# Who computes the low halves of the weight blocks: 32 subtractions from GpSimd to VectorE, and two pairs of blocks split later in their norm chain

## The chip, the cores and the metric

One NeuronCore of one Trainium2 chip runs the kernel. The metric is the device time of one execution in microseconds (us). The engines are TensorE (PE, matmuls; PEld its weight loads), VectorE (DVE), ScalarE (ACT), GpSimd (POOL) and SyncE (SP, which issues the loads). Each runs its own instructions in the order in which the program lists them and meets the others through semaphores.

## The reference

Two transformer blocks, all in fp32. The first is a trunk of two layers over 256 latent and 256 context tokens of width 1024:

```python
for i in range(DEPTH):                       # DEPTH = 2
    x, xc = trunk_layer(x, xc, mod, mod_c, p, ang_row, ang_col, last=(i == DEPTH - 1))

# trunk_layer
h = rmsnorm(x, p["g_pre_mix"]) * (1 + sc1) + sh1
u = h @ w_in
y = concatenate([y_sc, y_mla, y_cf, y_na], axis=-1) @ p["w_out"]
x = x + ga1 * rmsnorm(y, p["g_post_mix"])
hm = rmsnorm(x, p["g_pre_mlp"]) * (1 + sc2) + sh2
x = x + ga2 * rmsnorm(sq_relu_mlp(hm, p["w_mlp1"], p["w_mlp2"]), p["g_post_mlp"])
```

The four mixers are a short convolution (sc), a latent attention (mla), a convolution of 31 taps (cf, the "conformer") and an attention over a neighbourhood (na). The context rows xc go the same way in the first layer; in the last layer they give only keys and values. So layer 0 is wide (512 rows) and layer 1 narrow (256 rows). The second block (a differential attention, a dilated attention and a gated MLP) comes after it and is not touched here.

## The kernel before, in words

**Three products for one.** A matmul in fp32 is done as three of a faster type, fp32r: each operand is split into a high half H, the operand rounded to fp32r, and a low half L, operand minus H. `mm3` issues H·H (L430), L·H (L431) and H·L (L432). So every weight block has to be split before PE can use it, and every activation too.

**Weight blocks.** The weights lie in one stream of blocks of 128x1024, in the order of their use. SP fetches two at a time (1 MB, tile raw, four buffers). `step` (L355) takes the next block of the stream, lets ACT write H (L373) and then either POOL or DVE write L:

```python
nc.scalar.activation(hi, t[:, j, :], AF.Copy)
pool = pool or (self.pool_l and len(self.units) % self.pool_l == 0)
(nc.gpsimd if pool else nc.vector).tensor_tensor(lo, t[:, j, :], hi, op=ALU.subtract)
```

`self.pump(upto, pool)` calls `step` until the stream stands at block `upto`; `self.used` is the number of blocks that PE's instructions have taken up so far. What sets the order on an engine is where in the program `pump` is called: the subtraction stands behind all that the program wrote for its engine before.

**Attention** (`attention`, L1506) runs in slots, 19 in layer 0 and 11 in layer 1: one item (a head and 128 or 256 queries) enters per slot. A slot first pumps to `self.used + SLOT_LEAD`, then issues the item's scores and softmax (`attn_scores` or `na_scores`: scores S on PE, maxima mx and the bias nb = mx·nqs on DVE at L1403 and L1404, the exponentials P on ACT at L1412, their reciprocal sum rd and the multiply P·rd on DVE at L1414 and L1415), then the transposes of an earlier item (PT on PE, PTs copied by DVE and ACT), background taps of the convolution (cfacc: half the channels by DVE, L984, half by ACT, cft at L990, and POOL, L991), then "fillers" for PE (the nk, sc_x, sc_b, sc_c and out projections, matmuls that need a split weight block), then the values of the oldest item (PV; its halves yH on ACT, yL on DVE, L467 and L468; one y in layer 1). At slot 0 (`POOL_FROM = 0`) it sets `self.pool_l = 1`, from where on `step` gives every low half to POOL.

**Norm chains.** After the out projection and after the first MLP's second matmul, the rows 0 and 1 are normalized and turned into the operand of the next matmul: `pre_transpose` (L852) transposes xn in eight blocks (hT on PE), forms hF = hT·scale + shift on ACT (L843) or DVE (L845), and `pre_split` writes hH on ACT (L849) and hL on DVE (L850; `pool_free` is off here). After every second block it calls `between(k0)`. In the two wide chains (`block1_wide`, L1990 and L2023) `between` pumps two weight blocks, at k0 == 2, with `pool=ALL`.

**End of the first MLP** (L2035). After the chunks of m2 come in, `self.pool_l = 1` is set and `self.pump(self.used + 5)` splits the blocks of the next layer's first projection (tiles a, g, ag, tok). Later `conformer_in` sets `pool_l` itself between its two halves, and `token_block` clears it.

Of the kernel before, what the change touches and what calls it, by code (L numbers as in the profile page):

```python
# [38 lines left out]
ALL = (1,) * 8  # L39
# [17 lines left out]
TAPS = (3, 3), (4, 4)  # L57
TOK_TAPS = 3, 2
NORM_AT = 0
POOL_FROM = 0  # L60
CF_SLOTS = (7, 9, 12), (5, 7, 9)


# [240 lines left out]
class Program:  # L304
# [1206 lines left out]
    def attention(self, l, sets, y, fillers, steps):  # L1511


        items = [(kind, hd, st) for kind in ("mla", "na") for st in range(sets) for hd in range(4)]
        P, PT, bias, after = {}, {}, {}, []
        n = len(items)
        slots = n + AHEAD + 1
        total, done = sum(f[1] for f in fillers), 0.0
        for i in range(slots):
            if i == POOL_FROM:  # L1520
                self.pool_l = 1
            if fillers and fillers[0][4:]:
                for _, fn in [q for q in after if q[0] == "sc"]:
                    fn()
                after = [q for q in after if q[0] != "sc"]
            if i + 4 < n and items[i + 4][0] == "na" and items[i + 4][2] == 0 and i % 2 == 0:
                bias[i + 4] = [self.na_bias(l, items[i + 4][1] + e) for e in range(2)]
            if i + 1 in bias and i % 2:
                bias[i + 1] = bias[i + 2] = [f() for f in bias[i + 1]]
            self.pump(self.used + SLOT_LEAD)  # L1530
            if i < n:
                kind, *item = items[i]
                P[i] = self.attn_scores(*item) if kind == "mla" else self.na_scores(*item, bias.pop(i, None))
            if 0 <= i - AHEAD < n:
                PT[i - AHEAD] = (self.attn_transpose if items[i - AHEAD][0] == "mla" else self.na_transpose)(P.pop(i - AHEAD))
            self.background(*SLOT_TAPS[l])
            for _, fn in after:
                fn()
            after = []
            while fillers and (i == slots - 1 or fillers[0][2] <= i and all(x != fillers[0][3] for x, _ in after)  # L1540
                               and (done < total * (i + 1) / slots or not fillers[0][1])):
                fn, w, _, kind = fillers.pop(0)[:4]
                while any(x == kind for x, _ in after):
                    after.pop(0)[1]()
                r = fn()
                if r:
                    after.append((kind, r))
                done += w
            if i in steps:
                r = steps[i]()  # L1550
                if r:
                    after.append(("cf", r))
            k = i - AHEAD - 1
            if 0 <= k < n and items[k][0] == "na":
                self.na_values(*items[k][1:], PT.pop(k), y)
            elif 0 <= k < n and items[k][1] % 2:
                self.attn_values(*items[k][1:], [PT.pop(k - 1), PT.pop(k)], y)
            if k == 4 * sets - 1:
                self.KT = self.QT = self.VM = None
        for _, fn in after:  # L1560
            fn()
        self.pool_l = False
        assert not fillers
# [417 lines left out]
    def block1_wide(self, l, y, banks, ga):  # L1981
        v = self.nc.vector
        xn, n = {}, 0
        self.post_half(0, 0, banks.pop(0), ga[0])
        for p in self.out_second("out", OUT_ORDER, y, 4, 2):
            if p is None:
                h = self.new_h()
                self.pool_free = False
                self.pre_transpose([xn[0], xn[1]], *self.affine(l, 1, 0), h, 0,
                                   lambda k0: k0 == 2 and self.pump(self.used + 3, pool=ALL))  # L1990
                self.pool_free = True
                continue
            self.post_half(n, 1, p, ga[n // 2], (2, 3) if n > 1 else None)
            p = None
            if n < 2:
                self.post_end(n)
                xn[n] = self.pre_stats(n)[0]
            n += 1
            if n < 4:
                self.post_half(n, 0, banks.pop(0), ga[n // 2], (2, 3) if n > 1 else None)  # L2000
        self.pump(self.used + 5, pool=ALL)
        self.post_end(2, 3)
        xn[2], xn[3] = self.pre_stats(2, 3)
        ga = []

        hs, h = [h], None

        def ctx(between):
            self.pre_transpose([xn[2], xn[3]], *self.affine(l, 1, 1), hs[0], 256, between)

        n, held = 0, []

        def half(n, p):
            ps, y = p
            v.tensor_tensor(y, ps, y, op=ALU.add)
            self.post_half(n // 2, n % 2, y, ga[n // 4], (2, 3) if n > 3 else None)

        for p in self.mlp_wide(l, hs, ctx, lambda: ga.extend(self.gate_rows(l, 1, 2))):
            if p is None:
                h2 = self.new_h()  # L2020
                self.pool_free = False
                self.pre_transpose([xn[0], xn[1]], *self.affine(l + 1, 0, 0), h2, 0,
                                   lambda k0: k0 == 2 and self.pump(self.used + 3, pool=ALL))  # L2023
                self.pool_free = True
                continue
            if n < 5:
                half(n, p)
            else:
                held.append((n, p))
            p = None  # L2030
            if n in (1, 3):
                self.post_end(n // 2)
                xn[n // 2] = self.pre_stats(n // 2)[0]
            n += 1
        self.pool_l = 1  # L2035
        self.pump(self.used + 5)
        while held:
            half(*held.pop(0))

        def rows():  # L2040
            self.post_end(2, 3)
            xn[2], xn[3] = self.pre_stats(2, 3)

        self.ctx_rows = rows
        self.ctx_part = lambda: self.pre_transpose([xn[2], xn[3]], *self.affine(l + 1, 0, 1), h2, 256)
        return h2
# [438 lines left out]
```

## Time and profile before

| | |
|---|---|
| time, median of 3 runs | 1528.68 us (1526.71 to 1529.3) |
| the profiled execution's own time | 1518.72 us |
| its span, first to last instruction | 1516.8 us |
| mean granted clock of TensorE | 0.986 |
| PE busy | 1438.0 us (95%) |
| VectorE busy | 1030.6 us (68%) |
| ScalarE busy | 764.3 us (50%) |
| GpSimd busy | 566.5 us (37%) |
| low halves (L375) on VectorE | 197, 254.0 us |
| low halves (L375) on GpSimd | 117, 287.7 us |
| high halves (L373) on ScalarE | 314, 317.0 us |

A share is of the span. PE is the engine with hardly any free time, and it works in a fixed order: time is lost where its next instruction's operand is not there. The attention of layer 0 lies at about 133 to 262 us of the span, the first wide norm chain at 286 to 312, the second with the end of the first MLP at 676 to 720, the attention of layer 1 at 751 to 832. The granted clock is the share of TensorE's full speed (2.4 GHz) that the throttle allowed; its lower level is 1.2 GHz.

### The profile page before, as it was taken

Reading aid. Unit: us, or ns where it says so; the run is one execution under the profiler, and the core shown is the slowest. Engines: PE = TensorE matmul, PEld = TensorE weight load, DVE = VectorE, ACT = ScalarE, POOL = GpSimd, SP = SyncE. Lnnn points to the kernel's source line nnn. Section 1 sums busy time; section 2 is a strip of 40 time slices with the busy share of each in tenths; the row PEclk is TensorE's granted clock in tenths of the full one; section 3 lists DMA queues with packets and bytes.
Section 4 is the critical chain, followed back from the end, with each engine's and each line's share of the span. In section 5 each row is a group of like instructions: output and inputs, shape, how many; then the busy total and the mean of one; then the engine's idle time right before and its main releaser. Section 6 shows DMA issues by size and latency. Waiting matters only on the chain.

```text
span 1516.8 us, 21532 instructions
## 1 busy us (share of the span) xinstructions
PE 1438.0 (95%) x8284; PEld 1198.5 (79%) x8284; DVE 1030.6 (68%) x1636; ACT 764.3 (50%) x1398; POOL 566.5 (37%) x348
## 2 busy tenths in 40 slices
PE   8979999999989999998899999998999999899997
PEld 6756767888768878877677789986888998689896
DVE  5697673666988776788775665556566667756655
ACT  4445664565453223345666554454544663555553
POOL 2384631204543501016263400004022555737982
PEclk9999999999999999998999999999999999999999
DMA  9643621124444554634332455464645432644551
GB/s 339 226 176 139 139 102 72 56 84 166 158 171 172 196 169 179 214 137 146 95 74 97 145 182 192 169 203 162 211 167 171 140 134 86 216 137 161 189 185 56
DMA packets 72974, 235.64 MB, mean 155 GB/s; under 512 B 13472, under 2 KB 14120, under 8 KB 72872
## 3 DMA queue, kind: packets, MB, share of 16 engines
q1 hardware_dynamic: 72152, 233.58, 45.2%
q8 instruction: 65, 1.06, 0.3%
q10 hardware_dynamic: 720, 0.69, 0.1%
q14 instruction: 37, 0.30, 0.1%
HBM read 233.20 MB, written 1.05 MB: 154 GB/s over the span
## 4 chain that ended last, share of the span: by engine, by line
PE 65%; DVE 19%; ACT 8%; issue 5%; POOL 2%; DMA 1%; SPq 0%; DVEq 0%; ACTq 0%; POOLq 0%
PE m L431 7%; PE m L432 7%; PE m L430 7%; DVE L L375 3%; PE acc L430 3%; PE acc L431 3%; PE acc L432 3%; PE pj L430 2%; PE pj L431 2%; PE pj L432 2%; ACT H L373 2%; DVE cfacc L984 2%; POOL L L375 2%; PE up L432 2%; PE up L431 2%
## 5 line engine op out<-in xcount | busy, mean ns | idle before, releaser
L375 POOL TENSOR_TENSOR L<-raw,H 128x1024 fp32r<-128x1024 f32 x117 | 287.7, 2483 | 322.4 <-ACT H L373 303.8
L373 ACT ACTIVATE H<-raw 128x1024 fp32r<-128x1024 f32 x314 | 317.0, 1048 | 117.1 <-DMA raw<-in_wst 37.3
L375 DVE TENSOR_TENSOR L<-raw,H 128x1024 fp32r<-128x1024 f32 x197 | 254.0, 1317 | 73.6 <-ACT H L373 71.4
L367 POOL TENSOR_TENSOR uL<-raw,uH 128x512 fp32r<-128x512 f32 x32 | 46.3, 1478 | 193.5 <-ACT uH L366 193.4
L431 PE MATMUL m<-L,hidH 128*128 128x512 f32 x256 | 101.7, 397 | 9.7 <-DVE L L375 9.7
L431 PE MATMUL m<-hL,H 128*128 128x512 f32 (+1 forms) x304 | 108.6, 357 | 2.0 <-DVE hL L850 1.9
L432 PE MATMUL m<-hH,L 128*128 128x512 f32 (+1 forms) x304 | 108.4, 356 | 1.3 <-DVE L L375 1.3
L430 PE MATMUL m<-hH,H 128*128 128x512 f32 (+1 forms) x304 | 108.5, 357 | 1.0 <-ACT hH L849 1.0
L1771 ACT ACTIVATE rl<-m 128x512 f32<-128x512 f32 (+1 forms) x56 | 28.2, 504 | 152.5 <-PE m L432 152.5
L679 POOL TENSOR_TENSOR macc<-mt,macc 128x512 f32<-128x512 f32 x42 | 70.5, 1706 | 92.4 <-ACT mt L677 92.4
L430 PE MATMUL m<-H,hidH 128*128 128x512 f32 x256 | 101.3, 396 | 0.0
L432 PE MATMUL m<-H,hidL 128*128 128x512 f32 x256 | 100.3, 392 | 0.0
L1778 DVE TENSOR_TENSOR rl<-rl 128x512 f32<-128x512 f32 (+1 forms) x56 | 32.2, 575 | 93.1 <-ACT hid L1777 57.0
L683 DVE SCALAR_TENSOR_TENSOR macc<-raw,csil,macc 128x512 f32<-128x512 f32 x98 | 93.5, 1011 | 0.0
L991 POOL TENSOR_TENSOR cfacc<-cft,cfacc 128x512 f32<-128x512 f32 (+1 forms) x60 | 70.6, 1176 | 59.4 <-ACT cft L990 55.6
L432 PE MATMUL up<-h,L 128*128 128x256 f32 x288 | 81.7, 284 | 1.7 <-POOL L L375 1.7
L430 PE MATMUL up<-h,H 128*128 128x256 f32 x288 | 81.7, 284 | 0.0
L431 PE MATMUL up<-h,H 128*128 128x256 f32 x288 | 81.5, 283 | 0.0
L431 PEld LDWEIGHTS m<-L,hidH 128*128 128x128 f32 x256 | 48.4, 189 | 23.8 <-DVE L L375 14.2
L431 PEld LDWEIGHTS m<-hL,H 128*128 128x128 f32 x304 | 57.4, 189 | 10.8 <-DVE hL L850 2.6
L432 PEld LDWEIGHTS m<-hH,L 128*128 128x128 f32 x304 | 57.4, 189 | 10.3 <-DVE L L375 2.2
L430 PEld LDWEIGHTS m<-hH,H 128*128 128x128 f32 x304 | 57.4, 189 | 9.2 <-ACT hH L849 1.2
(533 smaller groups left out, 4112.3 us busy)
## 6 DMA issues: line engine op xcount, KB each, us to landing
raw<-in_wst SPq DMA_DIRECT2D x208, 1024.0 KB
mod<-in_wmod SPq DMA_DIRECT2D x16, 256.0 KB
X<-in_x SPq DMA_DIRECT2D x4, 512.0 KB
nab<-in_rpb SPq DMA_DIRECT2D x32, 64.0 KB
raw<-in_wst SPq DMA_DIRECT2D x2, 512.0 KB
wuq<-in_small SPq DMA_DIRECT2D x4, 256.0 KB
cst<-in_c SPq DMA_DIRECT2D x4, 256.0 KB
grow<-in_rows SPq DMA_DIRECT2D x4, 256.0 KB
```

Source lines behind the costliest of these rows:

```text
L367: nc.gpsimd.tensor_tensor(lo, src, hi, op=ALU.subtract)
L373: nc.scalar.activation(hi, t[:, j, :], AF.Copy)
L375: (nc.gpsimd if pool else nc.vector).tensor_tensor(lo, t[:, j, :], hi, op=ALU.subtract)
L430: mm(out, a[0], b[0], start=start, stop=False)
L431: mm(out, a[0], b[1], start=False, stop=False)
L432: mm(out, a[1], b[0], start=False, stop=stop)
L679: nc.gpsimd.tensor_tensor(o, t, o, op=ALU.add)
L683: v.scalar_tensor_tensor(o, a, c, o, op0=ALU.mult, op1=ALU.add)
L984: v.scalar_tensor_tensor(acc, src, w, acc, op0=ALU.mult, op1=ALU.add)
L991: nc.gpsimd.tensor_tensor(acc, t, acc, op=ALU.add)
L1771: nc.scalar.activation(r[:, :T], ps[:, :T], AF.Relu)
L1778: v.tensor_tensor(r[:, :T], r[:, :T], r[:, :T], op=ALU.mult)
```

## The change

`POOL_FROM` and the line that sets `pool_l` at slot 0 of each attention are removed: the low halves that `step` issues in the slots go to VectorE. In the two wide norm chains `between` pumps at k0 == 6, the last call, and not at k0 == 2, and without `pool=ALL`: ACT's two copies and the two subtractions come at the chain's end, the subtractions on VectorE. At the end of the first MLP `pool_l` is no longer set.

```diff
--- before.py
+++ after.py
@@ -57,7 +57,6 @@
 TAPS = (3, 3), (4, 4)
 TOK_TAPS = 3, 2
 NORM_AT = 0
-POOL_FROM = 0
 CF_SLOTS = (7, 9, 12), (5, 7, 9)
 
 
@@ -1517,8 +1516,6 @@
         slots = n + AHEAD + 1
         total, done = sum(f[1] for f in fillers), 0.0
         for i in range(slots):
-            if i == POOL_FROM:
-                self.pool_l = 1
             if fillers and fillers[0][4:]:
                 for _, fn in [q for q in after if q[0] == "sc"]:
                     fn()
@@ -1987,7 +1984,7 @@
                 h = self.new_h()
                 self.pool_free = False
                 self.pre_transpose([xn[0], xn[1]], *self.affine(l, 1, 0), h, 0,
-                                   lambda k0: k0 == 2 and self.pump(self.used + 3, pool=ALL))
+                                   lambda k0: k0 == 6 and self.pump(self.used + 3))
                 self.pool_free = True
                 continue
             self.post_half(n, 1, p, ga[n // 2], (2, 3) if n > 1 else None)
@@ -2020,7 +2017,7 @@
                 h2 = self.new_h()
                 self.pool_free = False
                 self.pre_transpose([xn[0], xn[1]], *self.affine(l + 1, 0, 0), h2, 0,
-                                   lambda k0: k0 == 2 and self.pump(self.used + 3, pool=ALL))
+                                   lambda k0: k0 == 6 and self.pump(self.used + 3))
                 self.pool_free = True
                 continue
             if n < 5:
@@ -2032,7 +2029,6 @@
                 self.post_end(n // 2)
                 xn[n // 2] = self.pre_stats(n // 2)[0]
             n += 1
-        self.pool_l = 1
         self.pump(self.used + 5)
         while held:
             half(*held.pop(0))
```

Counted by its instructions, 32 subtractions of 128x1024 go from POOL to DVE: 15 in the attention of layer 0, 2 in each norm chain, 3 at the end of the first MLP and at the convolution's first half after it, 10 in the attention of layer 1. The orders on PE and of SP's loads stay; ACT's changes in the two norm chains alone. The rows below have the line numbers of their own kernel; those of the changed kernel are one lower in the rows shown (L374 there is L375 in the profile).

VectorE in the attention of layer 0, two slots near its start (147.6 to 159.4 us of the span before). L, raw and H are a weight block's low half, its fetched form and its high half. Before:

```order
L1414 RECIPROCAL rd_1523<-den_1511 128x2
L1415 TENSOR_SCALAR P_1519<-P_1519,rd_1523 128x512
L984 SCALAR_TENSOR_TENSOR cfacc_886<-cfz_0_883,cfw_639,cfacc_886 128x512 x3
L1403 TENSOR_REDUCE mx_1595<-S_1598 128x1
L1403 TENSOR_REDUCE mx_1595<-S_1600 128x1
L1404 TENSOR_TENSOR nb_1596<-mx_1595,nqs_1320 128x2
L1414 RECIPROCAL rd_1609<-den_1597 128x2
L1415 TENSOR_SCALAR P_1605<-P_1605,rd_1609 128x512
L1490 COPY PTs_1625<-PT_1620 128x512
L984 SCALAR_TENSOR_TENSOR cfacc_886<-cfz_0_883,cfw_639,cfacc_886 128x512
```

and with the change:

```order
L1413 RECIPROCAL rd_1523<-den_1511 128x2
L1414 TENSOR_SCALAR P_1519<-P_1519,rd_1523 128x512
L374 TENSOR_TENSOR L_1537<-raw_1468,H_1536 128x1024
L374 TENSOR_TENSOR L_1547<-raw_1468,H_1546 128x1024
L983 SCALAR_TENSOR_TENSOR cfacc_886<-cfz_0_883,cfw_639,cfacc_886 128x512 x3
L374 TENSOR_TENSOR L_1592<-raw_1534,H_1591 128x1024
L1402 TENSOR_REDUCE mx_1595<-S_1598 128x1
L1402 TENSOR_REDUCE mx_1595<-S_1600 128x1
L1403 TENSOR_TENSOR nb_1596<-mx_1595,nqs_1320 128x2
L1413 RECIPROCAL rd_1609<-den_1597 128x2
L1414 TENSOR_SCALAR P_1605<-P_1605,rd_1609 128x512
L1489 COPY PTs_1625<-PT_1620 128x512
```

Three low halves have come in: two right behind the multiply P of one item and one right ahead of the maxima mx of the next. A fourth follows the last row shown.

VectorE in the attention of layer 0, at about 219 to 226 us. Before:

```order
L1201 SCALAR_TENSOR_TENSOR lns_2221<-lnth_2220,lns_2221 128x512
L650 TENSOR_TENSOR mr_3_2245<-mod_1529,brow 128x256
L468 TENSOR_TENSOR yL_1958<-PV_2259,yH_1957 128x256
L1437 TENSOR_REDUCE nb_2272<-S_2274 128x1
L1437 TENSOR_REDUCE nb_2272<-S_2275 128x1
L1414 RECIPROCAL rd_2286<-den_2273 128x2
```

and with the change:

```order
L1200 SCALAR_TENSOR_TENSOR lns_2221<-lnth_2220,lns_2221 128x512
L374 TENSOR_TENSOR L_2236<-raw_1890,H_2235 128x1024
L649 TENSOR_TENSOR mr_3_2245<-mod_1529,brow 128x256
L374 TENSOR_TENSOR L_2250<-raw_2059,H_2249 128x1024
L467 TENSOR_TENSOR yL_1958<-PV_2259,yH_1957 128x256
L374 TENSOR_TENSOR L_2267<-raw_2059,H_2266 128x1024
L1436 TENSOR_REDUCE nb_2272<-S_2274 128x1
L1436 TENSOR_REDUCE nb_2272<-S_2275 128x1
L1413 RECIPROCAL rd_2286<-den_2273 128x2
```

Two low halves stand ahead of yL, which the scores of a later item wait for, and one ahead of the reduces of the next softmax.

ScalarE in the first wide norm chain, with the high halves that VectorE's subtractions need (hF, hH: a block of the normalized rows and its high half). Before:

```order
L843 ACTIVATE hF_2869<-hT_2850,modT_3_2846,modT_4_1681 128x256
L849 ACTIVATE hH_2831<-hF_2865 128x256
L373 ACTIVATE H_2873<-raw_2247 128x1024
L373 ACTIVATE H_2877<-raw_2247 128x1024
L849 ACTIVATE hH_2833<-hF_2869 128x256
L843 ACTIVATE hF_2897<-hT_2884,modT_3_2846,modT_4_1681 128x256
L849 ACTIVATE hH_2835<-hF_2893 128x256
L849 ACTIVATE hH_2837<-hF_2897 128x256
L843 ACTIVATE hF_2905<-hT_2884,modT_3_2846,modT_4_1681 128x256
L849 ACTIVATE hH_2839<-hF_2901 128x256
L849 ACTIVATE hH_2841<-hF_2905 128x256
```

and with the change:

```order
L842 ACTIVATE hF_2869<-hT_2850,modT_3_2846,modT_4_1681 128x256
L848 ACTIVATE hH_2831<-hF_2865 128x256
L848 ACTIVATE hH_2833<-hF_2869 128x256
L842 ACTIVATE hF_2887<-hT_2874,modT_3_2846,modT_4_1681 128x256
L848 ACTIVATE hH_2835<-hF_2883 128x256
L848 ACTIVATE hH_2837<-hF_2887 128x256
L842 ACTIVATE hF_2895<-hT_2874,modT_3_2846,modT_4_1681 128x256
L848 ACTIVATE hH_2839<-hF_2891 128x256
L372 ACTIVATE H_2899<-raw_2247 128x1024
L372 ACTIVATE H_2903<-raw_2247 128x1024
L848 ACTIVATE hH_2841<-hF_2895 128x256
```

The two copies H have moved from the middle of the chain to the place right ahead of its last hH. On VectorE the two subtractions, which POOL had before, stand right ahead of the last hL in the same way.

## Rows read from the trace of the kernel before

**Rows 1.** The windows view: busy us of each engine, granted clock, DMA share and GB/s by stage.
```profile
core 0: us, PE busy (x) PEld busy (x) DVE busy (x) ACT busy (x) POOL busy (x), PEclk, DMA share, GB/s
133.00:262.00 129.00, 125.73 (x714) 88.86 (x713) 77.20 (x148) 76.58 (x155) 53.40 (x27) 0.99 0.38 110
286.00:312.00 26.00, 23.25 (x178) 21.86 (x176) 19.76 (x37) 13.12 (x31) 9.68 (x4) 1.00 0.24 82
676.00:720.00 44.00, 36.53 (x222) 33.42 (x221) 35.44 (x58) 24.19 (x53) 28.98 (x19) 0.88 0.36 126
751.00:832.00 81.00, 76.14 (x465) 57.51 (x466) 54.92 (x106) 51.48 (x104) 37.83 (x27) 0.98 0.35 85
```

**Rows 2.** Line L375 by engine: duration of one, ns, min/median/max.
```profile
L375 DVE TENSOR_TENSOR L<-raw,H x197: 1207/1218/3366, 19.3 to 1487.1; 128x1024 fp32r<-128x1024 f32 x197
...
L375 POOL TENSOR_TENSOR L<-raw,H x117: 2345/2408/3377, 139.9 to 1476.6; 128x1024 fp32r<-128x1024 f32 x117
```

**Rows 3.** Timeline of VectorE, attention of layer 0: start us, us, instruction [idle before <-releaser].
```profile
125.45 5.11 DVE L984 SCALAR_TENSOR_TENSOR cfacc<-cfz,cfw,cfacc 128x512 f32<-128x512 f32 x3
...
147.85 0.49 DVE L1415 TENSOR_SCALAR P<-P,rd 128x512 f32<-128x512 f32 x1
148.25 4.31 DVE L984 SCALAR_TENSOR_TENSOR cfacc<-cfz,cfw,cfacc 128x512 f32<-128x512 f32 x3
...
153.79 1.03 DVE L1404 TENSOR_TENSOR nb<-mx,nqs 128x2 f32<-128x2 f32 x1
...
160.07 1.65 DVE L757 SCALAR_TENSOR_TENSOR modT<-modT,pkt 128x8 f32<-128x8 f32 x2
...
168.12 0.16 DVE L1404 TENSOR_TENSOR nb<-mx,nqs 128x2 f32<-128x2 f32 x1
...
223.55 0.42 DVE L468 TENSOR_TENSOR yL<-PV,yH 128x256 fp32r<-128x256 f32 x1 [2.56 <-ACT yH L467]
```

**Rows 4.** Timeline of ScalarE, attention of layer 0.
```profile
148.40 1.99 ACT L373 ACTIVATE H<-raw 128x1024 fp32r<-128x1024 f32 x2
...
221.24 2.00 ACT L373 ACTIVATE H<-raw 128x1024 fp32r<-128x1024 f32 x2
```

**Rows 5.** Groups by form, VectorE 133 to 262: busy us, mean ns of one | idle before.
```profile
L1589 DVE SCALAR_TENSOR_TENSOR sccv<-scz,pkt,sccv 128x512 f32<-128x512 f32 x2 | 1.5, 752 | 1.6 <-ACT sccv L1588 1.6
```

**Rows 6.** What PE waits for, 133 to 262: us in total, times, longest.
```profile
PE S L1433 <- DVE yL L468: 1.4, 1, 1.4
PE sc_x L430 <- ACT P L1412: 0.8, 1, 0.8
```

**Rows 7.** Timeline of VectorE, attention of layer 1.
```profile
762.72 2.22 DVE L1404 TENSOR_TENSOR nb<-mx,nqs 128x2 f32<-128x2 f32 x1
...
788.01 1.72 DVE L1415 TENSOR_SCALAR P<-P,rd 128x512 f32<-128x512 f32 x1
...
793.04 3.12 DVE L1381 TENSOR_TENSOR nab<-nab,nam 128x512 f32<-128x512 f32 x2
```

**Rows 8.** What PE waits for, 751 to 832.
```profile
PE o L430 <- ACT y L467: 0.9, 1, 0.9
PE sc_c L430 <- ACT P L1412: 0.8, 1, 0.8
```

**Rows 9.** Timeline of VectorE, the two norm chains.
```profile
291.41 3.99 DVE L850 TENSOR_TENSOR hL<-hF,hH 128x256 fp32r<-128x256 f32 x2 [1.32 <-ACT hH L849]
...
679.96 3.95 DVE L850 TENSOR_TENSOR hL<-hF,hH 128x256 fp32r<-128x256 f32 x2 [1.32 <-ACT hH L849]
```

**Rows 10.** Timeline of GpSimd, the first norm chain.
```profile
290.20 4.91 POOL L375 TENSOR_TENSOR L<-raw,H 128x1024 fp32r<-128x1024 f32 x2 [30.43 <-ACT H L373]
```

**Rows 11.** What PE waits for, 286 to 312 and 676 to 720.
```profile
PE m L431 <- DVE hL L850: 1.9, 2, 1.5
...
PE tok L431 <- POOL L L375: 3.6, 2, 1.8
PE ag L431 <- DVE hL L850: 2.6, 2, 1.5
```

## The prediction

> **What bounds the kernel now.** I read the busy time by stage first, then the groups of the line that moves (L375, the low halves L), then the timelines of VectorE (DVE) and ScalarE (ACT) around it, and last what PE waits for. By stage [rows 1], PE is busy 125.73 of 129 us in the attention of layer 0 (133 to 262) and 76.14 of 81 in that of layer 1 (751 to 832): PE is the bound there, and a change shows only where an instruction in PE's fixed order comes late. In the two norm chains (286 to 312 and 676 to 720) PE has 2.75 and 7.47 us without work, and in the second its mean granted clock is 0.88. The chain there is transposes, norm halves (hF, hH, hL), then PE. DVE has room as a mean (77.20 of 129 in the first attention), but a mean tells nothing of where in a slot its instruction stands.
>
> One low half takes 1.218 us on DVE and 2.408 us on GpSimd (POOL) [rows 2]. So each of the 32 that move adds 1.22 us to DVE's queue and takes 2.41 us from POOL's. POOL's time is worth nothing by itself; its price is a hold: while POOL runs such an instruction, DVE instructions that read two SBUF operands stand still. The tiny nb at 153.79 takes 1.03 us, the one at 168.12, with POOL idle, 0.16; the 8-column modT takes 1.65 for two [rows 3]. The multiply P, a single-operand form, shows it too: 0.49 at 147.85 [rows 3], 1.72 at 788.01 [rows 7]. The Trainium skill, SBUF — State Buffer, "Who interferes with whom", says of this that DVE and GpSimd share one port pair under an exclusive lock; the trace agrees (0.16 against 1.03).
>
> **Attention, layer 0: 15 low halves.** Five lie in the stretch 138 to 164. They cost 5 x 1.22 = 6.1 us of DVE. Where one stands right behind P it also waits for its high half H: P starts at 147.85 [rows 3], and ACT begins the two H only at 148.40, 1.99 us for both [rows 4], so DVE would stand about 1.1 us, and that pattern comes three times (138.8, 148.4, 157.8): 3.2 us. What comes back is the holds: three nb (1.28, 1.03, 1.01) to 0.16 each, 2.84; one P at 156.72 from 0.98 to 0.49, 0.5; two modT, 1.3; and 0.46 us that DVE idles before modT [rows 3]. That is 6.1 + 3.2 - 2.84 - 0.5 - 1.3 - 0.46 = **+4.2 us**. Unknown is cfacc, seven multiply-adds of 128x512 on DVE, 4.31 us for three [rows 3]; POOL's own adds (its background taps) would now run earlier, beside other ones of the seven. At best they run like the same instruction form at L1589, 0.75 each [rows 5], which gives 7 x 0.69 = 4.8 back; at worst like the three at 125.45, beside POOL's adds, 5.11 [rows 3], 7 x 0.27 = 1.9 more. I take them unchanged, as POOL's adds stay: bounds -0.6 to +6.1. None of the 4.2 is covered, as PE's sc_x already waits 0.8 us for the exponential P that frees its bank [rows 6].
>
> Four more lie at 213 to 229. One (L_2181) stands before a softmax reduce, 1.2. Two stand before yL, which PE waits for now (1.4 us, [rows 6]): their H run 221.24 to 223.24 [rows 4], so the second low half ends at 222.24 + 2 x 1.22 = 224.68 and yL starts then and not at 223.55 [rows 3], 1.1. L_2267 stands before the next reduces, 1.2. Waits for H, half an ACT copy each for two of them, 0.9; one held P back, 0.5. Together **+3.9** (bounds 0, if PE's fillers cover it, to +5). The other six cost 7.3 us of DVE against about as much held time (nab, nb) and no PE wait of [rows 6] is laid to them: 0, with 3 either way.
>
> **Attention, layer 1: 10 low halves.** In its first slots two low halves (2.44) pay back an nb of 2.22 [rows 7] (2.06 more than 0.16): +0.4. One stands before the exponential that PE's sc_c waits for, 0.8 now [rows 8]: 1.22 and 0.3 of waiting, +1.5. Three between 784 and 798: 3.66 and 0.6 of waiting, minus the held P (1.72 to 0.49, 1.23) and the two nab, 3.12 now [rows 7] against 1.5 at the 0.75 of [rows 5], 1.6: +1.5. Two between 800 and 815, 2.44 and 1.1 of waiting, minus one held P, 0.7: +2.8, ahead of the o matmuls that wait for y already [rows 8]. The last two stand behind the last softmax reduce: 0. Sum **+6.2**, bounds 0 to +8.6 (those two in full); PE's 4.86 idle us here [rows 1] are these same waits and cover nothing.
>
> **Norm chains: 2 + 2 low halves, and ACT's copies with them.** Now POOL's pair takes 290.20 to 295.11 [rows 10] and DVE's two hL, 0.42 each where nothing holds them (yL has that shape [rows 3]), take 3.99; in the second chain 3.95 [rows 9]. PE waits for hL 1.9 and 2.6 us [rows 11]. After the change ACT's two copies and DVE's two low halves stand right ahead of the last hH and hL. In the first chain the hold goes; copies and low halves together (1.99 + 1.22, the second low half behind the second copy) come after the hL of the other seven blocks, while PE has the out matmuls and those seven blocks to run: the last hL is just in time, **-1.9**. Bounds -1.9 to +0.5 (the 2.4 of two low halves come out as a new wait). In the second, PE now stops for the held pair, in the middle of its eight blocks, with part of the stretch at 1.2 GHz; with the hold gone, the wait moves to the last block, about 2.4 us, with an eighth of the matmuls behind it: the wait of 2.6 goes, the slow stretch becomes shorter (0.88 over 44 us is 0.24 x 44 = 10.6 us at the low level, so at most 5.3 of loss), and the new wait comes in. Net **-3.0** with the three low halves at the end of the MLP included: they leave POOL, whose late low halves cost tok 3.6 [rows 11], and cost DVE 3.7 there. Bounds -6.2 (both waits gone) to 0. The fetches of weights keep their place in SP's queue; a raw buffer comes free up to some us later in a chain, and no ACT copy there waits for one.
>
> **Sum.** 4.2 + 3.9 + 0 + 6.2 - 1.9 - 3.0 = +9.4 us on the profiled execution of 1518.7, 1528.1. The profiled execution is 10.0 us under the median of the runs (1528.7), so on that scale **1538.1 us**. A measurement of this kernel tells about 0.2% (3.1 us) from no change.
>
> **The rivals.**
>
> *Faster (0.22).* The holds are worth more than the slots of DVE. It decides at one point: whether an L finds its H ready and DVE idle (DVE has 51.8 idle us of 129 [rows 1]), so that it ends before the next reduce's scores are there. Then the PE waits that come from held DVE instructions or POOL's late halves go: sc_x 0.8, yL 1.4 [rows 6], sc_c 0.8, o 0.9 [rows 8], hL 1.9 and 2.6, half of tok, 1.8 [rows 11]: -10.2, **1518.5**. For it: 2.41 against 1.22 us for the same work. Against it: in program order L stands directly ahead of reduces and behind the exponential, where DVE is waited for. The Trainium skill's GPSIMD Engine Reference, "Engine selection", says the same: elementwise work on two tiles belongs on VectorE, GPSIMD being about twice as slow. The ratio agrees with rows 2; what it says of the whole, no row shows.
>
> *No change (0.20).* Layer 0's attention hides its +8.1 behind PE's queue of fillers (125.73 of 129 busy), and layer 1's +6.2 stands against the -4.9 of the chains: +1.3, **1530.0**. For it: one PE wait of 1.4 and one of 0.8 are all that [rows 6] lists of weight in 129 us. Against: these very waits end at the instructions that come later.
>
> *Much slower (0.10).* Every L of both attentions is exposed with half an ACT copy of waiting, 25 x 1.22 + 25 x 0.5 = 43, less the 18.5 us of holds and idle time counted above and the chains' 4.9: +19.6, **1548.3**. PE would stop longer and drop to the low clock more often.
>
> That the change does not do what it says is not open: its order of instructions has the 32 rows on DVE.
>
> **Numbers.** Forecast 0.48, faster 0.22, no change 0.20, much slower 0.10. The forecast's own range, with the bounds in mind, is 1532 to 1546. To leave out no more than 2 in 10, the range reaches into the faster case at 1519 and to 1547 above. Faster by over 0.2%: 0.22; within: 0.20; slower: 0.58.
>
> **What would show it.** Right: the line L375 has 32 fewer on POOL and more on DVE; nb falls to about 0.16 in both attentions; PE's waits for P (L1412) and yL grow in 138 to 164 and 213 to 229, and layer 1's attention grows by some 6 us; the pairs of hL fall from 4 to 0.8 us; a single wait for the last hL stands in the second chain. Wrong: both attentions as long as now, with DVE idle less before rd; or cfacc of 0.75 us each, which would pay for the low halves; or a tok wait that stays at 3.6 with DVE as the releaser.

## The result and the profile after

The changed kernel took 1538.41 us (median of 4 runs, 1536.94 to 1540.99) beside 1528.09 for the kernel before: 10.3 us more, a ratio of 1.0079, 95% interval 1.0059 to 1.0099. Forecast was 1538.1.

The profiled execution lasted 1536.94 us (span 1535.1, mean granted clock 0.980); that of before 1518.72 at 0.986. So the two traces differ by 18.2 us where the runs differ by 10.3. The execution of before was a quick one: a second one took 1521.6 us, and 28 timed runs of before beside the first experiments have a mean clock of 0.980 and a median of 1526.6. Differences of single traces are read with that in mind, and ratios come from the runs. Two runs of all those below, one of the kernel before (3252.9 us) and one of k7_pool_at6 (1769.8), lie far from the rest and enter no figure here.

Both traces have the same 8284 matmuls in the same order. The start of the same one in both shows where time is gained and lost (stages by the times of before):

| stage | forecast, us | traces, us |
|---|---|---|
| up to the attention, 0 to 133 | 0 | +1.5 |
| attention of layer 0, 133 to 262 | +8.1 | +12.8 |
| first norm chain, 262 to 312 | -1.9 | -2.2 |
| MLP, 312 to 676 | 0 | +2.1 |
| second chain, end of the MLP, projections, 676 to 751 | -3.0 | -2.5 |
| attention of layer 1 and its end, 751 to 860 | +6.2 | +6.5 |
| the rest | 0 | +0.2 |

The stages in the windows view of the changed kernel, shifted by these offsets (they answer to [rows 1]):

```profile
core 0: us, PE busy (x) PEld busy (x) DVE busy (x) ACT busy (x) POOL busy (x), PEclk, DMA share, GB/s
134.50:276.20 141.70, 130.17 (x714) 91.10 (x713) 85.29 (x164) 76.73 (x155) 18.27 (x12) 0.95 0.36 104
300.20:324.00 23.80, 22.91 (x178) 21.72 (x176) 19.63 (x39) 13.33 (x31) 4.77 (x2) 1.00 0.26 89
690.10:730.50 40.40, 34.49 (x223) 31.91 (x222) 33.60 (x64) 24.59 (x54) 16.79 (x14) 0.94 0.39 137
762.60:850.10 87.50, 78.14 (x465) 58.76 (x466) 62.22 (x116) 51.71 (x104) 15.46 (x17) 0.96 0.31 78
```

The moved line, by engine (beside [rows 2]). It is L374 here, as the lines of the changed kernel behind the removed constant are one or more lower:

```profile
L374 DVE TENSOR_TENSOR L<-raw,H x229: 1208/1219/2643, 20.0 to 1505.4; 128x1024 fp32r<-128x1024 f32 x115
...
L374 POOL TENSOR_TENSOR L<-raw,H x85: 2357/2412/3395, 309.9 to 1494.9; 128x1024 fp32r<-128x1024 f32 x85
```

229 on VectorE and 85 on GpSimd, 32 each way, and the time of one is as before, 1.219 and 2.412 us. In the first attention GpSimd falls from 53.40 to 18.27 us, VectorE rises only from 77.20 to 85.29, and PE has 11.5 us without work (141.70 less 130.17) where it had 3.3, at a clock of 0.95 and not 0.99. In the stage of the second chain the clock is 0.94 where it was 0.88.

**The first slots of layer 0's attention.** VectorE's timeline there (beside [rows 3]):

```profile
141.36 1.23 DVE L374 TENSOR_TENSOR L<-raw,H 128x1024 fp32r<-128x1024 f32 x1 [1.15 <-ACT H L372]
...
142.84 4.82 DVE L983 SCALAR_TENSOR_TENSOR cfacc<-cfz,cfw,cfacc 128x512 f32<-128x512 f32 x3
...
148.89 0.16 DVE L1403 TENSOR_TENSOR nb<-mx,nqs 128x2 f32<-128x2 f32 x1
...
152.71 2.36 DVE L374 TENSOR_TENSOR L<-raw,H 128x1024 fp32r<-128x1024 f32 x2 [1.14 <-ACT H L372]
154.99 5.18 DVE L983 SCALAR_TENSOR_TENSOR cfacc<-cfz,cfw,cfacc 128x512 f32<-128x512 f32 x3
160.09 1.21 DVE L374 TENSOR_TENSOR L<-raw,H 128x1024 fp32r<-128x1024 f32 x1
...
166.78 1.23 DVE L374 TENSOR_TENSOR L<-raw,H 128x1024 fp32r<-128x1024 f32 x1 [1.10 <-ACT H L372]
167.92 1.75 DVE L983 SCALAR_TENSOR_TENSOR cfacc<-cfz,cfw,cfacc 128x512 f32<-128x512 f32 x1
...
169.79 1.12 DVE L756 SCALAR_TENSOR_TENSOR modT<-modT,pkt 128x8 f32<-128x8 f32 x2
```

and GpSimd's adds in the second of these slots:

```profile
154.38 5.24 POOL L990 TENSOR_TENSOR cfacc<-cft,cfacc 128x512 f32<-128x512 f32 x3 [7.28 <-ACT cft L989]
```

nb takes 0.16 (it had 1.01 to 1.28), as forecast. The brackets of three low halves are the waits for H: 1.15, 1.14, 1.10, together 3.39 (forecast 3.2). The low halves take 1.23 + 2.36 + 1.21 + 1.23 = 6.03. But cfacc takes 4.82, 5.18 and 1.75, 11.75 for seven, where it took 9.81: with the low halves gone from its queue, GpSimd runs its adds (154.38 to 159.62) beside just these instructions. In the kernel before, the cfacc that started at 148.25 ran beside GpSimd's low halves, and the adds came behind them, from 154.77:

```profile
149.53 5.28 POOL L375 TENSOR_TENSOR L<-raw,H 128x1024 fp32r<-128x1024 f32 x2 [2.36 <-ACT H L373]
```

So cfacc was held all the same before, by the very instructions that moved; the adds have taken their place. What PE waited for in this attention, and two matmuls of its sc_x:

```profile
PE PT L1483 <- DVE modT L752: 2.6, 1, 2.6
PE PV L1467 <- DVE mr L649: 2.3, 1, 2.3
PE S L1432 <- ACT P L1411: 1.8, 1, 1.8
PE S L1399 <- ACT P L1411: 1.5, 1, 1.5
PE sc_x L429 <- ACT P L1411: 1.4, 1, 1.4
...
PE S L1432 <- DVE yL L467: 0.4, 1, 0.4
```

```profile
173.91 0.63 PE L430 MATMUL sc_x<-hL,H 128*128 128x512 f32 x1
...
176.66 0.39 PE L431 MATMUL sc_x<-hH,L 128*128 128x512 f32 x1
```

The waits on the exponential P and on what stands behind it in VectorE's queue (modT, mr) are new or longer. After a PE stall of 2.6 and one of 1.4 us the matmul takes 0.63 us at 173.91 and 0.39 at 176.66, which is the low and the high level of the clock (granted 0.50 from 173.9 to 176, 1.00 from 177 to 180). One matmul follows the other by 0.43 us at the low level and by 0.23 at the high one.

By the starts of the matmuls, the 12.8 us of this attention are 6.9 of waiting in the first slots, 1.4 of the low clock right behind them, 3.8 of waiting at 213 to 229 (in the times of before) and 0.7 of the low clock behind that.

**At 223 to 240**, where before yL started at 223.55:

```profile
233.34 1.22 DVE L374 TENSOR_TENSOR L<-raw,H 128x1024 fp32r<-128x1024 f32 x1 [1.68 <-ACT H L372]
...
234.82 1.22 DVE L374 TENSOR_TENSOR L<-raw,H 128x1024 fp32r<-128x1024 f32 x1
235.95 0.42 DVE L467 TENSOR_TENSOR yL<-PV,yH 128x256 fp32r<-128x256 f32 x1
```

yL comes as soon as the two low halves are over, at 235.95. The high half yH that it needs was there at 234.52 (ScalarE, 234.16 and 0.36), so it is 1.4 us late; 1.1 was forecast. But PE does not pay at that place: it waits for yL 0.4 us, and had waited 1.4 before. By the profile it has stood 2.3 us already for mr, which VectorE does right behind the first low half and that one's 1.68 us of waiting for H.

**Norm chains.** VectorE in the first one, and PE's waits in both (beside [rows 9, 11]):

```profile
307.11 2.36 DVE L374 TENSOR_TENSOR L<-raw,H 128x1024 fp32r<-128x1024 f32 x2 [0.53 <-ACT H L372]
309.39 0.42 DVE L849 TENSOR_TENSOR hL<-hF,hH 128x256 fp32r<-128x256 f32 x1
```

```profile
PE m L430 <- DVE hL L849: 0.2, 1, 0.2
...
PE ag L430 <- DVE hL L849: 1.1, 1, 1.1
...
PE tok L430 <- POOL L L374: 0.5, 1, 0.5
```

The hL pair of 3.99 us has become single hL of about 0.42, the two low halves end right ahead of the last of them, and PE waits 0.2 us for it. In the second chain PE waits once, 1.1, and tok for GpSimd 0.5 where it was 3.6.

**Attention of layer 1**, VectorE and PE's waits (beside [rows 7, 8]):

```profile
776.49 0.16 DVE L1403 TENSOR_TENSOR nb<-mx,nqs 128x2 f32<-128x2 f32 x1
...
798.61 3.47 DVE L374 TENSOR_TENSOR L<-raw,H 128x1024 fp32r<-128x1024 f32 x2 [0.70 <-ACT H L372]
...
804.53 0.48 DVE L1414 TENSOR_SCALAR P<-P,rd 128x512 f32<-128x512 f32 x1
...
807.94 1.28 DVE L1380 TENSOR_TENSOR nab<-nab,nam 128x512 f32<-128x512 f32 x2
```

```profile
PE sc_c L429 <- ACT P L1411: 2.5, 1, 2.5
...
PE o L429 <- ACT y L466: 1.7, 2, 1.4
```

nb went from 2.22 to 0.16, P from 1.72 to 0.48, the two nab from 3.12 to 1.28. The two low halves at 798.61 take 3.47 and not 2.44, again beside GpSimd's adds, and sc_c waits 2.5 for the exponential (0.8 before), o 1.7 for y (0.9).

### The profile page after: what moved, and what is told of

Same layout as the page of the kernel before. It is cut to its first block, busy times and chain, and to the rows that moved or that the text cites. A ratio compares the mean times of both kernels' runs of the same rounds, so it can differ in the third digit from the quotient of the medians.

```text
span 1535.1 us, 21501 instructions
## 1 busy us (share of the span) xinstructions
PE 1447.6 (94%) x8284; PEld 1204.2 (78%) x8284; DVE 1043.7 (68%) x1668; ACT 765.2 (50%) x1398; POOL 490.4 (32%) x316
## 4 chain that ended last, share of the span: by engine, by line
PE 60%; DVE 21%; ACT 9%; issue 6%; POOL 3%; DMA 1%; SPq 0%; DVEq 0%; ACTq 0%; POOLq 0%
PE m L430 7%; PE m L431 7%; PE m L429 7%; DVE L L374 5%; POOL L L374 3%; PE acc L429 3%; PE acc L430 2%; PE acc L431 2%; PE pj L430 2%; PE pj L429 2%; PE pj L431 2%; DVE cfacc L983 2%; ACT H L372 2%; PE up L431 2%; PE up L430 1%
## 5 line engine op out<-in xcount | busy, mean ns | idle before, releaser
L374 DVE TENSOR_TENSOR L<-raw,H 128x1024 fp32r<-128x1024 f32 x229 | 292.5, 1303 | 84.1 <-ACT H L372 82.0
L374 POOL TENSOR_TENSOR L<-raw,H 128x1024 fp32r<-128x1024 f32 x85 | 208.0, 2475 | 329.4 <-ACT H L372 310.8
L990 POOL TENSOR_TENSOR cfacc<-cft,cfacc 128x512 f32<-128x512 f32 (+1 forms) x60 | 74.4, 1239 | 100.2 <-ACT cft L989 96.3
L983 DVE SCALAR_TENSOR_TENSOR cfacc<-cfz,cfw,cfacc 128x512 f32<-128x512 f32 (+1 forms) x60 | 64.2, 1070 | 1.5
```

Of the source, the lines that this page charges most:

```text
L983: v.scalar_tensor_tensor(acc, src, w, acc, op0=ALU.mult, op1=ALU.add)
L990: nc.gpsimd.tensor_tensor(acc, t, acc, op=ALU.add)
```

## The experiments

Twelve kernels. The clock column is the mean over a kernel's runs of (1 - granted clock) x span: what the low level took at most, as a matmul there takes about twice as long (0.43 us for 0.23); for the kernel before it is 30 to 31 us. It is a bound and no share of the time: it also counts the low level while PE waits for an operand. In the attention of layer 0 it is 7.1 us in the trace of the change (0.05 of 141.7) and 1.3 before (0.01 of 129), 5.8 more, where the starts of the matmuls show 2.1 lost by the clock.

| run | median, us | ratio to before, 95% | clock, us |
|---|---|---|---|
| the change | 1538.4 | 1.0079, 1.0059 to 1.0099 | 34.2 |
| k0_same | 1527.2 | 0.9999, 0.9982 to 1.0015 | 31.7 |
| k1_attn0 | 1536.1 | 1.0072, 1.0047 to 1.0097 | 37.4 |
| k2_attn1 | 1530.0 | 1.0029, 1.0016 to 1.0043 | 29.7 |
| k3_chains_end | 1524.0 | 0.9980, 0.9962 to 0.9997 | 31.8 |
| k5_chains_only | 1524.9 | 0.9979, 0.9968 to 0.9990 | 33.6 |
| k6_dve_at2 | 1523.3 | 0.9974, 0.9962 to 0.9987 | 29.0 |
| k7_pool_at6 | 1522.3 | 0.9976, 0.9960 to 0.9993 | 29.3 |
| k8_idle | 1515.2 | 0.9916, 0.9901 to 0.9931 | 24.5 |
| k9_idle_alone | 1521.3 | 0.9966, 0.9955 to 0.9977 | 28.7 |
| k10_noadd | 1531.1 | 1.0033, 1.0019 to 1.0047 | 30.7 |
| k11_idle_twice | 1540.6 | 1.0089, 1.0068 to 1.0110 | 33.4 |
| k12_behind | 1528.2 | 1.0012, 0.9999 to 1.0025 | 28.7 |

### The parts, one by one

**k0_same**: no edit.

> 

> The kernel before, unchanged: a control, and a second profile of it. Its profiled execution on record (1518.7 us) lies some 9 us under the median of its timed runs (1528.1). Theory A (the first profile was a lucky one, and the 18 us by which the two profiles differ are partly of that): a second profile of it is some us longer, and shows in which stage; the ratio is 1.000 within its interval. Theory B (profiled executions are shorter than timed ones whenever the same kernel is taken): again about 1519, ratio 1.000.

Ratio 0.9999; the second profiled execution took 1521.6 us at a clock of 0.982, the ten runs of this kernel 1521.6 to 1529.6. That is 2.8 us longer than the first, 2.1 of them before the attention begins, 0.5 in that of layer 0 and -1.1 in that of layer 1 (so much do two executions of one kernel differ by stage). So theory A has the direction and little of the size; two profiles don't tell it from theory B.

**k1_attn0** and **k2_attn1**: one attention each with its low halves on VectorE.

```diff
-            if i == POOL_FROM:
+            if i == POOL_FROM and l == 1:      (k1_attn0)
+            if i == POOL_FROM and l == 0:      (k2_attn1)
```

> 

> Only the 15 low halves of layer 0's attention on VectorE, all else as before. Theory (the sum of the prediction, mended by the two profiles: the low halves and the waits for their high halves stand in front of the softmax, 6.9 us in its first slots and 3 to 4.5 later, plus a stretch of the low clock): +8 to +12 us over before, 0.5 to 0.8%. Rival (PE's fillers cover it and the 12.8 us between the profiles are of the execution): within 2 us of before.

> 

> Only the 10 low halves of layer 1's attention on VectorE. Theory (the sum of the prediction): +6.2 us, and the two profiles differ by 6.5 in this stage: +0.4%. Rival (the held nb, P and nab that POOL lets go pay for it): 0, within 2 us of before.

+0.72%, 11.0 us (7.2 to 14.8), and +0.29%, 4.4 us (2.4 to 6.6): both attentions cost, neither is hidden. The rival that the fillers cover layer 0 falls. The clock column is 7.0 us higher in k1_attn0 (37.4 beside 30.4) and not in k2_attn1 (29.7).

**k3_chains_end**: the two lines with `k0 == 6`, and `pool_l = 1` gone at the end of the first MLP; attentions as before.

> 

> Only the two wide norm chains (two blocks split at the chain's end, low halves on VectorE) and the three low halves at the end of the first MLP; both attentions as before. Theory (the sum of the prediction): -1.9 and -3.0, -4.9 us; the two profiles differ by -2.2 and -2.5 there: -0.3%, faster than both kernels. Rival (the waits only move to the last hL and to tok): 0, within 2 us of before.

-0.20%, 3.1 us (0.5 to 5.8): faster than both kernels, though the interval reaches into the rival's 2 us. The three parts add up: 0.72 + 0.29 - 0.20 = 0.81, measured together 0.79.

### The chains

**k5_chains_only**, **k6_dve_at2**, **k7_pool_at6**:

```diff
-                                   lambda k0: k0 == 2 and self.pump(self.used + 3, pool=ALL))
+                                   lambda k0: k0 == 6 and self.pump(self.used + 3))            (k5)
+                                   lambda k0: k0 == 2 and self.pump(self.used + 3))            (k6)
+                                   lambda k0: k0 == 6 and self.pump(self.used + 3, pool=ALL))  (k7)
```

> 

> Only the two wide norm chains changed (split at the chain's end on VectorE); the end of the first MLP and both attentions as before. Theory: the chains carry the gain of 3 us that the earlier run with the end of the MLP showed, -0.1 to -0.2%; the PE wait tok <- POOL L of 3.6 us stays. Rival (the gain is the end of the MLP's): within 0.05% of before.

> 

> In the two chains the two low halves on VectorE, but split where they were before, at the chain's middle. Theory (POOL's hold of hL is what PE waits for): the pair of hL falls from 4 to 0.8 us, but two low halves of 2.4 us and their wait for H stand ahead of the hL of the second half, so PE's wait in the chain stays at about 2 us: 0 to -1 us. Rival (the engine alone matters, not the place): the same gain as at the chain's end, -2 us or more in the stages 286 to 312 and 676 to 690.

> 

> In the two chains the two blocks split at the chain's end, but the low halves left on POOL. Theory (the hold needs POOL's low half beside an hL): POOL now starts only with the last hH, and holds at most the last hL, 2.4 to 4.8 us, and the work behind it: PE waits once, for the last hL; about 0. Rival (the place alone matters): hL free of holds, the same gain as with VectorE, -2 us in each stage.

k5 is -0.21%, as much as with the end of the MLP; its tok still waits for GpSimd:

```profile
PE tok L431 <- POOL L L375: 3.3, 2, 2.0
```

so these 3.3 us of wait are worth nothing that the runs can tell. The traces show that PE gives the larger part back one step later, and not all. Counted from 676 us, the tok matmuls at 707 come 7.7 us earlier than before in k3_chains_end and 2.8 in k5_chains_only; at 720 it is 4.0 and 1.9. PE has overtaken the context rows, whose xn is ready 4.0 us earlier by that count, and not 7.7. Of the 4.9 us by which the end of the MLP puts k3_chains_end ahead, 2.1 stay.

The theories said 0 to -1 for k6 and k7, and both came out at -0.24 to -0.26%: missed. VectorE in the first chain of k6, then of k7:

```profile
291.55 2.36 DVE L375 TENSOR_TENSOR L<-raw,H 128x1024 fp32r<-128x1024 f32 x2 [0.53 <-ACT H L373]
...
296.22 0.76 DVE L850 TENSOR_TENSOR hL<-hF,hH 128x256 fp32r<-128x256 f32 x2
```

```profile
296.91 1.49 DVE L850 TENSOR_TENSOR hL<-hF,hH 128x256 fp32r<-128x256 f32 x1 [1.77 <-ACT hH L849]
```

Either edit alone ends the hold of 4 us: in k6 the hL are 0.42 and 0.38 us each, behind two low halves that VectorE does in 2.36; in k7 GpSimd's pair touches only the last hL, 1.49. By the starts of the matmuls the first chain gains 2.2 (k5), 1.5 (k6) and 0.4 us (k7; 1.0 up to the transposes at 310 us), and the second, up to 720 us, 1.9, 1.4 and 2.2. The order in the first chain is what the theory says, the second chain has another one. The gains of k6 and k7 are larger than the theory's, and the ratios of the runs (intervals of 0.1 to 0.2% either way) don't tell the three apart.

### The place in VectorE's order

**k8_idle**: the changed kernel, but `step` puts a low half of the attentions on a list, and `softmax` takes one from it:

```diff
+            else:
+                self.defer.append((len(self.units), self.next_entry, lo, t[:, j, :], hi))
...
         rd = self.sm("rd", 2)
+        self.low()
         v.reciprocal(rd, den)
```

`take` issues what is still on the list of the block that it hands out, and the raw buffer is held until then.

> 

> The changed kernel, with the 25 low halves of both attentions kept on VectorE but issued one per softmax between the bias nb and the reciprocal rd, where VectorE idles about 1.75 us for the exponential (a low half is 1.22 us), and never in front of maxima or behind a copy H that is not done. Theory (it is the place in VectorE's order, the 1.1 us waits for H and the 1.2 us ahead of the maxima, that costs the 11 us and 4 us of the two attentions, not the work): both costs go, the holds of nb and P stay away, and the kernel is at least as fast as the one with only the chains changed, 0.4 to 0.7% faster than before (1517 to 1521). Rival (VectorE's extra 37 us of work, or its collisions with POOL's adds, cost by themselves): slower than before still, by 0.2 to 0.5%.

-0.84%, 1515.2 us: 23 us less than with the change, 12.8 less than before, with the very same 32 low halves on VectorE. Of the 25 on the list 21 stand between nb and rd in the trace, and 4 at the ends of the attentions. A slot of its VectorE:

```profile
147.26 1.21 DVE L394 TENSOR_TENSOR L<-raw,H 128x1024 fp32r<-128x1024 f32 x1
149.09 0.17 DVE L1431 RECIPROCAL rd<-den 128x2 f32<-128x2 f32 x1 [0.62 <-ACT P L1428]
...
149.76 2.32 DVE L1000 SCALAR_TENSOR_TENSOR cfacc<-cfz,cfw,cfacc 128x512 f32<-128x512 f32 x3
```

L stands where VectorE waited 1.75 us for the exponential; 0.62 of that is left before rd. And cfacc takes 0.77 each, because it starts ahead of GpSimd's adds (152.67). In the whole attention of layer 0, PE's largest wait for an operand of VectorE is 1.0; that for yL, 1.4 before, is 0.4:

```profile
PE nk L448 <- DVE L L394: 1.0, 1, 1.0
...
PE S L1450 <- DVE yL L484: 0.4, 1, 0.4
```

By the starts of the matmuls the attention of layer 0, 12.8 us longer with the change, is as long as before (-0.1), and that of layer 1 is 3.4 us shorter. So the place takes the whole cost away in layer 0, and a gain over before comes in layer 1 alone; together with the chains and the end of the MLP (4.6) that makes 8.1 of the 12.8 us of the runs. These traces do not place the rest, as that of before is the quick one (clock column 21.2, and 22.7 in that of k8_idle).

**k9_idle_alone**: the same with chains and MLP end as before.

> 

> The kernel before with only the two attentions changed: their 25 low halves on VectorE, one per softmax, between nb and rd; norm chains and the end of the first MLP as before. Theory (place, not work; and the effects of the stages add): the run with the changed chains too was 0.84% faster than before, of which the chains gave 0.20%; so 0.6% faster here, about 1518. Rival (the two edits need each other): within 0.3% of before.

-0.34%, half of what was expected. With the chains' 0.20 that gives 0.54 (0.33 to 0.75 by the two intervals), measured together is 0.84 (0.69 to 0.99). So the excess is hardly clear of the noise. If it is real, it goes with the clock column: 31.0 falls to 24.5 with both, to 28.7 with the attentions alone and not at all (31.8) with chains and MLP end alone. By the traces the edits do not help each other's waits: the attentions stand much alike in k9_idle_alone (layer 0 +1.1, layer 1 -3.4) and in k8_idle (-0.1, -3.4). Why the clock would be higher with both, no run here tells.

**k12_behind**: as k8_idle, but the list is emptied behind the slot's fillers.

```diff
+            self.low(100)
             if i in steps:
```

> 

> The changed kernel with the 25 low halves on VectorE, each issued behind the fillers of its slot: no longer right behind P, where it waits for its H (1.1 us each time), but still ahead of the next slot's maxima. Theory (of the 6.9 us in the first slots 3.4 are waits for H and the rest the work itself, 1.22 each): about 4 to 7 us less than with the change, 1531 to 1534. Rival 1 (the waits for H are all that costs): as the variant between nb and rd, 1515 to 1519. Rival 2 (a low half ahead of the maxima costs all, its wait nothing): 1537 to 1540, as with the change.

1528.2: 10.2 us less than with the change, more than the 4 to 7 of the theory, and 13 us above k8_idle. Both rivals fall: the waits for H are not all that costs, and the work ahead of the maxima is not all either. VectorE in the first two slots:

```profile
143.97 2.31 DVE L394 TENSOR_TENSOR L<-raw,H 128x1024 fp32r<-128x1024 f32 x1
...
147.51 1.28 DVE L1420 TENSOR_TENSOR nb<-mx,nqs 128x2 f32<-128x2 f32 x1
...
151.22 2.32 DVE L1000 SCALAR_TENSOR_TENSOR cfacc<-cfz,cfw,cfacc 128x512 f32<-128x512 f32 x3
153.45 3.44 DVE L394 TENSOR_TENSOR L<-raw,H 128x1024 fp32r<-128x1024 f32 x2
```

No bracket at the low halves, cfacc at 0.77; but now GpSimd's adds stand beside the low halves (2.31 for one, 3.44 and not 2.36 for two) and beside the first nb, 1.28. So this run does not price the waits for H by themselves: what runs beside the adds changed with the place.

**k11_idle_twice**: k8_idle with every such low half issued twice.

> 

> The fast variant (one low half per softmax between nb and rd, chains changed) with every such low half issued twice, the second one writing the same values again: 25 x 1.22 us more of VectorE. Theory (the place between nb and rd has about 1.75 us in the latent attention's softmaxes and 0.92 in the other's, so one low half is free and a second is not): 0.7 us for each of some 11, 1.2 for each of some 14, up to 24 us, of which PE's fillers cover some: 10 to 20 us over the variant's 1515. Rival (VectorE has room anyway, and the gain came from POOL's holds alone): within 4 us of the variant.

25.4 us over k8_idle, above the 10 to 20 that were expected and near the 24 of the theory with nothing covered; the rival's 4 falls, and VectorE has no room for the second one. By the starts of the matmuls 10.0 of it lie in the attention of layer 0 and 13.6 in that of layer 1, where 3.4 come at its end, behind the last softmax. Part of it came by another way than the gap before rd: the low halves themselves are late for PE (1.0 in k8_idle):

```profile
PE nk L449 <- DVE L L395: 2.3, 1, 2.3
...
PE sc_c L449 <- DVE L L395: 0.8, 1, 0.8
```

**k10_noadd**: the changed kernel without 12 of GpSimd's adds.

```diff
-                nc.gpsimd.tensor_tensor(acc, t, acc, op=ALU.add)
+                if l or not self.in_attn:
+                    nc.gpsimd.tensor_tensor(acc, t, acc, op=ALU.add)
```

> 

> The changed kernel without POOL's 12 adds to cfacc in the attention of layer 0: the convolution leaves out these taps for half of the channels. Theory (the seven multiply-adds cfacc on VectorE, 9.8 us before and 11.7 us after the change in the first slots, are lengthened by POOL's adds beside them): cfacc falls to about 0.75 us each, 5.3 us for seven, and layer 0's attention gets 6 us shorter than with the change, 1531 to 1533 in all. Rival (they are that long by themselves): cfacc as in the changed kernel, 1.4 to 1.7 us each, the time within 2 us of it.

1531.1, 7.3 us less than with the change, as expected; this kernel leaves out these taps of the convolution. cfacc in the three slots:

```profile
143.26 2.31 DVE L984 SCALAR_TENSOR_TENSOR cfacc<-cfz,cfw,cfacc 128x512 f32<-128x512 f32 x3
...
152.91 2.32 DVE L984 SCALAR_TENSOR_TENSOR cfacc<-cfz,cfw,cfacc 128x512 f32<-128x512 f32 x3
...
162.99 0.75 DVE L984 SCALAR_TENSOR_TENSOR cfacc<-cfz,cfw,cfacc 128x512 f32<-128x512 f32 x1
```

0.75 to 0.77 each, 5.38 for seven beside 11.75: the 6.4 us are GpSimd's adds. The rival, that cfacc is that long by itself, falls. The Trainium skill, SBUF — State Buffer, "Who interferes with whom", has the rule (one shared port pair, held by one of the two engines at a time), and these rows agree with it. The two low halves of k12_behind at 3.44 us and not 2.36 are the same thing.

## Why the prediction came out right, and where it was off

**The time and the mechanism** were right: VectorE's queue in the attentions costs more than the holds give back, the chains gain, and the sum is 10.3 where 9.4 was worked out. By the parts alone it is less good, as the errors go both ways: layer 0 +11.0 (forecast +8.1), layer 1 +4.4 (+6.2), chains and MLP end -3.1 (-4.9). That the forecast of 1538.1 and the measured 1538.4 lie so close is in part luck.

**Layer 0, first slots: +4.2 forecast, 6.9 in the trace** (the exponential of the fourth item starts 8.33 us later, the first 1.47). It lies above the bound of 6.1. Five of the terms stand: low halves 6.03 (6.1), waits for H 3.39 (3.2), nb -2.84 (-2.84), P -0.5 (-0.5), idle time ahead of modT -0.46 (-0.46). Two were mis-sized. cfacc was taken "unchanged, as POOL's adds stay"; it came out at its upper bound, +1.94 of 1.9. The adds stay, but in the kernel before it was GpSimd's low halves that stood beside most of cfacc, and held the adds back; they went, and the adds moved to where cfacc runs. modT gave back 0.5 and not 1.3, for the same reason (an add beside it). With both, the sum is 7.0.

**Layer 0, 213 to 229: +3.9 forecast**, 3.5 in the trace at the transposes' copy PTs (12.96 us late, after 9.5 before this stretch). The size came out, the wait not: PE's wait for yL was to grow and fell from 1.4 to 0.4 us, as PE had stood for mr (2.3 us) before. The prediction has no wait for mr; that the sum fits in spite of it is luck in part.

**In the attentions the clock was not in the sum.** The prediction counted it in the second chain, and in the attentions only in the "much slower" case. In the trace it adds 2.1 us to the waits of layer 0. In the change's runs the clock column is 34.2 us, 4 more than for before, and in k1_attn0 7 more: part of layer 0's excess over the forecast, how large a part the runs do not say. This also weakens the use of one trace: that of before lay 9 us under the median of its runs, and its clock column is 21.2 us and not 30 to 31.

**Layer 1: +6.2** came out at 4.4 (2.4 to 6.6) in the runs, which does not exclude it, and at 6.5 in the traces. nb, P and nab gave back what was forecast or more (nab 1.84 for 1.6), and low halves beside GpSimd's adds cost about 2 us that the 1.22 each left out.

**The chains: -1.9 and -3.0** are -2.2 and -2.5 in the trace; the runs give -3.1 (0.5 to 5.8) for both. The hold was the reason, as k5, k6 and k7 show from three sides. The new wait for the last hL in the second chain was put at 2.4 and is 1.1. The -3.0 has no full sum in the prediction: how much of the slow clock's 5.3 would go was left open. The clock there rose from 0.88 to 0.94, so the bound of 5.3 became 2.4 (0.06 of 40.4). Of the wait of tok, which the bounds counted at 3.6, the traces keep about 2, as PE meets the context rows behind it.

**The rivals.** Faster: it named the point, "whether an L finds its H ready and DVE idle", and there it fails in this kernel, while k8_idle, where both hold for 21 of 25, is 1515.2, near that rival's 1518.5. The Trainium skill's GPSIMD Engine Reference, "Engine selection", puts elementwise work on two tiles on VectorE, GPSIMD being about twice as slow. It is borne out in k8_idle and not in the change itself: the ratio for one instruction says nothing of its place. No change: layer 0 was not hidden. Much slower: not every low half was exposed.

## What to carry to other kernels

Moving work to the faster engine is a change of order on that engine: price what stands right behind each moved instruction and whether its own operand is there yet. Look for the engine's idle time within its chain (here 1.75 us in each softmax of the latent attention, while ScalarE computes the exponential, and 0.92 in the other's) and put the work there, one piece per gap; the same 32 low halves on VectorE were 0.79% slower with 25 of them in one place and 0.84% faster with these in another. When an instruction leaves a queue, ask also what moves up in its stead and what that will then run beside.

## What was not expected of the hardware

Stalls of PE can cost more than their length. In the attention of layer 0 the clock fell at PE's stalls of 2.6 and 1.4 us, and again at those of 2.3 and 1.8, and the matmuls at the low level lost 2.1 us more. How much this makes over the whole kernel is open: the clock column, a bound, differs by 9.7 us (34.2 beside 24.5) between the change and k8_idle, which differ by 23.2, and by 7.0 for k1_attn0, which is 11.0 slower. But it is no higher for k2_attn1 (29.7), 4.4 us slower than before, and higher for k5_chains_only (33.6), which is faster.

And VectorE's cfacc, 1.4 us each in the kernel before, takes 0.75 where no GpSimd instruction runs beside it, so half of its time there was the other engine: its low halves before the change, its adds with it.
